# A two-layer decoder step on one core: the indexer's key tile first, unscaled values, and a head's key products in three PSUM banks

## Chip, cores and metric

One core of a Trainium2 chip runs the whole step in one launch. The metric is device time in microseconds (us), the median of several executions.

## What is computed

Two layers work on 512 prompt tokens and 8 samples of 4 new tokens (544 columns in all; 1024 channels, f32). Layer 0 mixes tokens by indexer-sparse attention, layer 1 by retention, and an MLP with squared relu follows each. Only layer 0's attention is touched by the change:

```python
z = h @ w_in                                   # 1024 -> 1024 q, 256 k, 256 v, 256 qi, 64 ki, 4 wi
q = rms_norm(q, q_gain); k = rms_norm(k, k_gain)
idx = jnp.einsum('thd,sd->ths', qi, ki)        # the indexer: 4 heads of 64
score = jnp.einsum('th,ths->ts', wi, relu(idx))
score = jnp.where(causal, score, -jnp.inf)
_, sel = lax.top_k(score, topk)                # topk = 128 keys of each query
logits = q . k[sel] * 128 ** -0.5 + bias       # 8 query heads on 2 key/value groups
y = (softmax(logits) @ v[sel]) @ w_out
```

`h` is the RMS-normed input, so each column (token) of the projection carries a factor r = rsqrt(mean square). The kernel multiplies by r after the projection, or leaves it out where a later norm removes it (queries and keys).

## The kernel before

**Dense tiles.** The projection gives transposed results: a tile holds 128 output channels (partitions) by 544 tokens, as two banks of 272 columns. f32 products are made from high and low parts (`wh`, `wl`, `xh`, `xl`; three products), so one tile is 8 steps of 6 matmuls, 48 in all (L506). The high part of a weight is made by ScalarE (L465), the low part by VectorE or, for keys, values and the first four query tiles, by GpSimd (L466). Tiles lie in the PSUM ring `mm`, which has two buffers of two banks. `ps_a` and `ps_b` have two buffers of one bank each.

**Order of the tiles.** The call at the end (`run(dense8(...) ...)`, L1174) lists them: two tiles of indexer queries (`ev_qi`), one narrow tile of 68 channels with the indexer's keys and head weights (`ev_kw`), two of keys (`ev_k`), two of values (`ev_v`), four of queries; after `settle()` a second `run(queries(1))` adds the other four queries. That makes 15 tiles, or 720 matmuls.

**What lies between them.** While `run` issues a tile it advances generators in a list `side`. `ev_kw` puts three of them there when the keys have been spread (L739) and transposed (L744): `ranks` (`scores`: the products L759 on TensorE, relu by ScalarE L762, weighted sum on VectorE L765 and L767), `deferred` (the samples' scores, L810 to L853) and `picks` (`select`: 16 rounds of MAX8 and MATCH_REPLACE on VectorE for each of three query blocks, L780 and L781). The samples' own selection, L865 to L871, has 16 rounds and a last one. All of it ends in the masks `nmask` and `nsel`.

**Values and keys.** `ev_v` multiplies the PSUM tile by r on VectorE (L914, `hs<-mm,RB`), TensorE transposes it (L897, L898) and ScalarE copies it to tokens (L899, L900). `ev_k` goes through `head_norm`, whose last VectorE product (L891) releases the transposes of the keys.

**Heads.** After the query tiles VectorE computes the query norms' reciprocal (L966), from which GpSimd and ScalarE make additive masks (L999, L1002), and `dq` (L969) for the samples' queries (L975, L977). `softmax` makes for each head four key products, one for each block of 128 queries, 512 to 128 keys wide (L1014); VectorE adds the mask and takes the row maximum out of PSUM (L1015), then L1017, the exponential on ScalarE (L1018), L1019 and L1020. `values` transposes the weights (L1030) and multiplies them with the values (L1041).

**Who sets the order.** The generators and the call's list only propose; a scheduler places every instruction when the program is built, from priorities and from buffers coming free. After that each engine runs its own fixed list. The chip sees nothing of the generators.

Of the kernel before, what the change touches and what calls it, by code (L numbers as in the profile page):

```python
# [26 lines left out]
FT = mybir.dt.float32  # L27
# [117 lines left out]
def decoder_step(ctx, tc, x_prompt, x_sample, cache_k, cache_v, cache_kidx, state_ret, page_table,  # L145
# [55 lines left out]
    def two(ap):  # L201
        return ap.rearrange("p (c n) -> p c n", c=2)
# [127 lines left out]

    def rsqrt_columns(x, n):
        return rsqrt(x, [tmp.tile([128, 20], FT, name=m)[:, :n] for m in ("rsy", "rsa")])

# [36 lines left out]
    def finish_norm(columns, then):  # L370
        if columns:
            ps = token_sums(acc)
            V.tensor_scalar(v1[:, :5], ps[:, :5], 1.0 / D, EPS, op0=OP.mult, op1=OP.add)
            r = rsqrt_columns(v1[:, :5], 5)
        else:
            r = row_rsqrt([acc] + late, D)
            late.clear()
        for _ in range(3):
            yield
        if columns:  # L380
            a, b = spread(r)
            A.activation(RB[:, :512], a, AF.Copy)
            V.tensor_copy(RB[:, 512:], b)
        else:
            spread_rows(r, RB)
        norm["pending"] = False
        if then:
            yield
            then()

    def start_norm(columns=False, then=None):
        norm["pending"] = True
        follow.append(finish_norm(columns, then))
# [103 lines left out]
    def tile_of(hl, xs, t, m, evac, i):  # L497
# [3 lines left out]
        for k in range(n):  # L501
# [8 lines left out]
            if k % 2:  # L510
                if k == n - 1:
                    if norm["pending"]:
                        z = PS["main"].tile([128, T], FT, name="early", tag=PS["early"][0], bufs=PS["early"][1])
                        A.activation(two(z), halves(ps), AF.Copy)
                        ps = z
# [152 lines left out]
    if True:  # L668
# [18 lines left out]
        SY.dma_start(ptab, page_table.rearrange("b n -> (b n)").rearrange("(o n) -> o n", o=1))  # L687
        start_norm(columns=True)

# [33 lines left out]
        def ev_qi(i, ps):  # L723
            V.tensor_tensor(two(qiT[i]), halves(ps), two(RB), op=OP.mult)
            yield
            for s in range(2):
                pq = ps_b()
# [6 lines left out]
        def ev_kw(i, ps):  # L734
# [13 lines left out]
            SY.dma_start(kidx_sample[0].rearrange("b t d -> (b t) d"), kitok[:NS, 4, :64])  # L748
            side.append([ranks, 2.0, 0.0])
            side.append([deferred, 0.7, 0.0])  # L750
            side.append([picks, 1.0, 0.0])

# [140 lines left out]

        def to_tokens(src, dst):
            pa, pb = ps_a(), ps_b()
            for b in range(4):
                PE.transpose(pa[:, 128 * b:128 * (b + 1)], src[:, 128 * b:128 * (b + 1)], ident)  # L897
            PE.transpose(pb[:NS, :128], src[:, SP:], ident)  # L898
            A.activation(dst[:, :4, :], pa.rearrange("p (b d) -> p b d", b=4), AF.Copy)  # L899
            A.activation(dst[:NS, 4, :], pb[:NS, :128], AF.Copy)  # L900

# [10 lines left out]
        def ev_v(g, ps):  # L912
            z = hs_tile(FT)
            V.tensor_tensor(two(z), halves(ps), two(RB), op=OP.mult)  # L914
            yield
            to_tokens(z, vtok[:, :, 128 * g:128 * (g + 1)])
            if g:
# [66 lines left out]
        def prompt_heads(hs):  # L984
# [19 lines left out]
            def softmax(h):  # L1004
                s = H[h]
                mx = tmp.tile([128, 4], FT, name="mx")
                sm = tmp.tile([128, 4], FT, name="sm")
                r = QR[h // 4][0][:, h % 4, :]
                for blk in (3, 2, 1, 0):
                    W = 128 * (blk + 1)  # L1010
                    c = slice(blk, blk + 1)
                    P = s["P"][blk]
                    ps = ps_a()
                    PE.matmul(ps[:, :W], qT[h][:, 128 * blk:128 * (blk + 1)], kT[h // 4][:, :W], start=True, stop=True)  # L1014
# [152 lines left out]
        def queries(g):  # L1167
# [5 lines left out]
        side.append([early, 0.7, 0.0])  # L1173
        run(dense8(w_in, 1536, 256, ev_qi) + dense8(w_in, 1792, 68, ev_kw, m=68) + dense8(w_in, 1024, 256, ev_k, eng=G)  # L1174
            + dense8(w_in, 1280, 256, ev_v, eng=G) + queries(0))
# [428 lines left out]
```

## Time and profile before

| | |
|---|---|
| median of 3 runs | 1584.08 us (1580.71 to 1584.30) |
| profiled execution, its own time | 1581.1 us |
| its span | 1579.2 us, mean granted clock 0.992 |
| PE (TensorE) busy | 1527.9 us, 97% |
| DVE (VectorE) busy | 1059.9 us, 67% |
| ACT (ScalarE) busy | 611.9 us, 39% |
| POOL (GpSimd) busy | 190.5 us, 12% |

Line numbers (L...) are those of this kernel. In rows that group instructions a following xN is their number; a product of plain f32 operands counts as two, a transpose or a split product as one. A bracket at a row's end gives the engine's idle time before it and what ended that. Time runs from the start of the span; the attention of layer 0 lies in the first 245 us.

### The profile page before, as it was taken

The page shows a single profiled execution, that of the slowest core. Times are in us where ns is not written, and L with a number is a line of the kernel's source. Part 1 is how long each engine was busy: PE and PEld are TensorE (multiplying, and loading weights), DVE is VectorE, ACT ScalarE, POOL GpSimd, SP SyncE. Part 2 cuts the span into 40 slices and gives each one's busy share as a digit, 9 for nine tenths or more (in the row PEclk, how much of TensorE's full clock was granted, in tenths as well). Part 3 has the DMA queues.
Part 4 walks back from the last instruction along what each step waited for, and adds up shares of the span by engine and source line. Part 5 has one row for each costly group of instructions (what it writes and reads, how often), then busy time and mean ns, then how long its engine had stood idle before and what let it go on. Part 6 is the DMA issues. An engine that isn't in the chain of part 4 may idle for free.

```text
span 1579.2 us, 28176 instructions
## 1 busy us (share of the span) xinstructions
PE 1527.9 (97%) x11670; PEld 1440.2 (91%) x11670; DVE 1059.9 (67%) x1950; ACT 611.9 (39%) x1036; POOL 190.5 (12%) x172
## 2 busy tenths in 40 slices
PE   7989899999999999999999999999998999999998
PEld 6689559899999999999899999999988999999998
DVE  6599774778677676556566465565568687677653
ACT  4423663545444444423232232223236454444432
POOL 3220320100000000212221122121210000000000
PEclk9999999999999999999999999999999999999999
DMA  6533252222332233223724622722812322332211
GB/s 177 156 98 94 71 185 81 81 81 81 107 107 86 82 101 107 79 79 109 246 67 163 197 84 91 260 71 73 274 60 64 105 83 82 107 107 82 83 51 57
DMA packets 135774, 172.53 MB, mean 109 GB/s; under 512 B 11660, under 2 KB 92630, under 8 KB 135646
## 3 DMA queue, kind: packets, MB, share of 16 engines
q1 hardware_dynamic: 135578, 170.72, 33.3%
q8 instruction: 91, 1.49, 0.4%
q14 instruction: 37, 0.30, 0.1%
q10 hardware_dynamic: 68, 0.02, 0.0%
HBM read 148.34 MB, written 25.01 MB: 110 GB/s over the span
## 4 chain that ended last, share of the span: by engine, by line
PE 87%; DVE 8%; DMA 2%; ACT 2%; issue 1%; SPq 0%; DVEq 0%; ACTq 0%
PE mm L506 56%; PE mm L570 16%; PE pa L570 2%; PE pb L1487 2%; PE pb L1513 1%; PE pa L1431 1%; DMA raw<-in_mlp_w_in_dram 1%; PE pa L1457 1%; DVE wl L466 1%; PE pb L1468 1%; PE pa L1041 1%; DVE sc L781 1%; PE pa L1014 1%; DVE m L780 1%; PE pb L1100 1%
## 5 line engine op out<-in xcount | busy, mean ns | idle before, releaser
L506 PE MATMUL mm<-xs,wh 128*128 128x272 f32 (+1 forms) x2784 | 501.4, 295 | 13.5 <-ACT r L1209 5.9
L506 PEld LDWEIGHTS mm<-xs,wh 128*128 128x128 f32 (+1 forms) x2784 | 410.0, 190 | 27.5 <-issue 8.9
L506 PE MATMUL mm<-hs,wh 128*128 128x272 f32 x2304 | 393.4, 289 | 3.2 <-DVE x L656 2.0
L506 PEld LDWEIGHTS mm<-hs,wh 128*128 128x128 f32 x2304 | 329.6, 189 | 5.5 <-DVE x L656 2.6
L465 ACT ACTIVATE wh<-raw 128x1024 fp32r<-128x1024 f32 x159 | 167.9, 1057 | 382.0 <-PE mm L506 356.9
L506 PE MATMUL mm<-xs,wl 128*128 128x272 f32 (+1 forms) x1392 | 297.5, 292 | 0.0
L570 PE MATMUL mm<-xs,sh 128*128 128x272 f32 x1344 | 259.1, 289 | 3.1 <-ACT r L583 1.8
L506 PE MATMUL mm<-hs,wl 128*128 128x272 f32 x1152 | 241.1, 288 | 0.0
L656 DVE TENSOR_TENSOR x<-mm,x 128x544 f32<-128x544 f32 x176 | 127.0, 723 | 163.4 <-PE mm L506 162.1
L506 PEld LDWEIGHTS mm<-xs,wl 128*128 128x128 f32 (+1 forms) x1392 | 222.7, 190 | 3.0 <-issue 1.1
L570 PEld LDWEIGHTS mm<-xs,sh 128*128 128x128 f32 x1344 | 210.3, 188 | 5.8 <-ACT r L586 3.5
L466 DVE TENSOR_TENSOR wl<-raw,wh 128x1024 fp32r<-128x1024 f32 x151 | 188.7, 1250 | 16.9 <-ACT wh L465 9.3
L570 PE MATMUL mm<-xs,sl 128*128 128x272 f32 x672 | 192.8, 287 | 0.0
L506 PEld LDWEIGHTS mm<-hs,wl 128*128 128x128 f32 x1152 | 182.1, 188 | 0.2
L570 PEld LDWEIGHTS mm<-xs,sl 128*128 128x128 f32 x672 | 126.3, 188 | 0.0
L662 ACT ACTIVATE sh<-ss 128x512 fp32r<-128x512 f32 x112 | 70.6, 630 | 123.8 <-PE mm L570 118.7
L663 DVE TENSOR_TENSOR sl<-ss,sh 128x512 fp32r<-128x512 f32 x112 | 76.7, 686 | 16.2 <-PE mm L570 16.2
L662 ACT ACTIVATE sh<-raw 128x512 fp32r<-128x512 f32 x84 | 53.1, 632 | 88.2 <-PE mm L570 70.8
L663 DVE TENSOR_TENSOR sl<-raw,sh 128x512 fp32r<-128x512 f32 x84 | 58.6, 698 | 9.3 <-PE mm L570 9.3
L1470 DVE SCALAR_TENSOR_TENSOR raw<-raw,pb 128x512 f32<-128x512 f32 x64 | 43.3, 684 | 24.9 <-PE pb L1468 15.8
L663 DVE TENSOR_TENSOR hs<-r,hs 128x544 fp32r<-128x544 f32 x64 | 46.1, 720 | 16.0 <-ACT hs L662 15.8
L412 POOL COPY acc<-sq 128x544 f32<-128x544 f32 x4 | 3.1, 780 | 444.8 <-ACT sq L408 444.8
(345 smaller groups left out, 1814.6 us busy)
## 6 DMA issues: line engine op xcount, KB each, us to landing
raw<-in_mlp_w_in_dram SPq DMA_DIRECT2D x32, 1024.0 KB
raw<-in_mlp_w_out_dram SPq DMA_DIRECT2D x32, 1024.0 KB
raw<-in_ret_w_in_dram SPq DMA_DIRECT2D x24, 1024.0 KB
raw<-in_state_ret_dram SPq DMA_DIRECT2D x32, 512.0 KB
out_dram<-raw SPq DMA_DIRECT2D x32, 512.0 KB
raw<-in_ret_w_out_dram SPq DMA_DIRECT2D x8, 1024.0 KB
raw<-in_att_w_in_dram SPq DMA_DIRECT2D x7, 1024.0 KB
raw<-in_cache_k_dram SPq DMA_DIRECT2D x32, 128.0 KB
```

The source lines that it names most:

```text
L465: A.activation(h, view, AF.Copy)
L466: eng.tensor_tensor(l, view, h.bitcast(FT), op=OP.subtract)
L506: PE.matmul(ps[:m, c, :HALF], w[:, k, m * t:m * (t + 1)], x[c] if isinstance(x, tuple) else x[:, HALF * c:HALF * (c + 1)], start=(k == 0 a ...
L570: PE.matmul(ps, a[:, i, :], b, start=(first and i == 0 and j == 0), stop=(i == 3 and j == 2), skip_group_check=True)
L656: V.tensor_tensor(two(xT[m]), halves(ps), two(xT[m]), op=OP.add)
L662: A.activation(dst_h, src, AF.Copy)
L663: V.tensor_tensor(dst_l, src, dst_h.bitcast(FT), op=OP.subtract)
L780: V.max(out=m8, in_=sc)
L781: V.match_replace(out=sc, in_to_replace=m8, in_values=sc, imm_value=TAKEN)
L1014: PE.matmul(ps[:, :W], qT[h][:, 128 * blk:128 * (blk + 1)], kT[h // 4][:, :W], start=True, stop=True)
L1470: V.scalar_tensor_tensor(sl, sl, gam4[h], pu, op0=OP.mult, op1=OP.add)
L1487: PE.matmul(ps[:, SP - WJ[j]:], v[:, j, 128 * e:128 * (e + 1)], a[:, AM[j]:AM[j] + WJ[j]], start=(j == 0 and v is vh and a is am[0]), stop ...
```

## The change

1. The token factor r of the first norm, as a column (`rsqrt_columns`), gets a tile of its own (`rcol`) that stays.
2. The narrow tile `ev_kw` is listed ahead of the two `ev_qi` tiles, and `ranks`, `deferred` and `picks` are put into `side` by the second of these.
3. `ev_v` copies the PSUM tile on ScalarE without the factor; after the transpose a token is a partition, so the factor is a scale of ScalarE's copy to tokens: five operations (four blocks and the samples) in place of two.
4. The four key products of a head lie in one `mm` buffer (blocks 3 and 2, a bank each) and one `ps_a` buffer (blocks 1 and 0 in one bank) instead of four `ps_a` buffers.

```diff
     def finish_norm(columns, then):
...
-            r = rsqrt_columns(v1[:, :5], 5)
+            r = rsqrt_columns(v1[:, :5], 5, columns)
...
-        start_norm(columns=True)
+        rcol = ap.tile([128, 5], FT, name="rcol")
+        start_norm(columns=rcol)
...
         def ev_qi(i, ps):
             V.tensor_tensor(two(qiT[i]), halves(ps), two(RB), op=OP.mult)
             yield
+            if i:
+                side.append([ranks, 2.0, 0.0])
+                side.append([deferred, 0.7, 0.0])
+                side.append([picks, 1.0, 0.0])
...
             SY.dma_start(kidx_sample[0].rearrange("b t d -> (b t) d"), kitok[:NS, 4, :64])
-            side.append([ranks, 2.0, 0.0])
-            side.append([deferred, 0.7, 0.0])
-            side.append([picks, 1.0, 0.0])
...
-        def to_tokens(src, dst):
+        def to_tokens(src, dst, scale=None):
...
-            A.activation(dst[:, :4, :], pa.rearrange("p (b d) -> p b d", b=4), AF.Copy)
-            A.activation(dst[:NS, 4, :], pb[:NS, :128], AF.Copy)
+            if scale is None:
+                A.activation(dst[:, :4, :], pa.rearrange("p (b d) -> p b d", b=4), AF.Copy)
+                A.activation(dst[:NS, 4, :], pb[:NS, :128], AF.Copy)
+                return
+            for b in range(4):
+                A.activation(dst[:, b, :], pa[:, 128 * b:128 * (b + 1)], AF.Identity, scale=scale[:, b:b + 1])
+            A.activation(dst[:NS, 4, :], pb[:NS, :128], AF.Identity, scale=scale[:NS, 4:5])
...
         def ev_v(g, ps):
             z = hs_tile(FT)
-            V.tensor_tensor(two(z), halves(ps), two(RB), op=OP.mult)
+            A.activation(two(z), halves(ps), AF.Copy)
             yield
-            to_tokens(z, vtok[:, :, 128 * g:128 * (g + 1)])
+            to_tokens(z, vtok[:, :, 128 * g:128 * (g + 1)], rcol)
...
+                pm, pq = ps_mm(), ps_a()
+                banks = {3: pm[:, 0, :512], 2: pm[:, 1, :384], 1: pq[:, :256], 0: pq[:, 256:384]}
                 for blk in (3, 2, 1, 0):
...
-                    ps = ps_a()
+                    ps = banks[blk]
...
-        run(dense8(w_in, 1536, 256, ev_qi) + dense8(w_in, 1792, 68, ev_kw, m=68) + dense8(w_in, 1024, 256, ev_k, eng=G)
+        run(dense8(w_in, 1792, 68, ev_kw, m=68) + dense8(w_in, 1536, 256, ev_qi) + dense8(w_in, 1024, 256, ev_k, eng=G)
```

The lists of instructions as placed, in three places. A name such as `mm_735` is one buffer of the ring `mm`; "waits" names the engine whose semaphore an instruction waits for. Lines of the changed kernel are a little higher: L507 is L506 before, L735 is L729, L762 is L759, L868 to L874 are L865 to L871, L974 and L977 are L966 and L969, L983 is L975, L985 is L977, L1024 and L1025 are L1014 and L1015, L1040 is L1030.

TensorE, the first scores. Before (the tile `mm_735` is the first of the keys, and the scores follow its end):

```order
L506 MATMUL mm_735<-xs_229,wh_481 128x272 x2
L506 MATMUL mm_735<-xs_230,wh_481 128x272 x2
L506 MATMUL mm_735<-xs_229,wl_482 128x272 x2
L506 MATMUL mm_735<-xs_244,wh_481 128x272 x2
L506 MATMUL mm_735<-xs_245,wh_481 128x272 x2
L506 MATMUL mm_735<-xs_244,wl_482 128x272 x2
L759 MATMUL pa_719<-hs_259,hs_256 128x512
L759 MATMUL pa_724<-hs_259,hs_256 128x512
```

Now (`mm_598` is the second tile of indexer queries):

```order
L507 MATMUL mm_598<-xs_244,wh_342 128x272 x2
L507 MATMUL mm_598<-xs_245,wh_342 128x272 x2
L507 MATMUL mm_598<-xs_244,wl_343 128x272 x2
L735 MATMUL pb_572<-hs_257,ca_126 128x32
L762 MATMUL pa_719<-hs_260,hs_257 128x512
L762 MATMUL pa_724<-hs_260,hs_257 128x512
L507 MATMUL mm_735<-xs_139,wh_491 128x272
```

The scores stand ahead of the first key tile instead of behind it: 144 dense matmuls come before the first score where 192 did.

VectorE, the end of the selection. Before:

```order
L865 MAX s_268<-ss 32x8
L966 RECIPROCAL qi_1688<-qr_1676 128x20
L969 TENSOR_TENSOR dq<-ident,qr_1676 32x128
L866 MATCH_REPLACE ss<-s_268,ss 32x544
L868 MAX s_268<-ss 32x8
L869 MEMSET s_268 32x7
L870 MATCH_REPLACE ss<-s_268,ss 32x552
L871 TENSOR_SCALAR nsel<-ss 32x544
L977 TENSOR_TENSOR Qs_275<-hs,pb 128x8x4 x4
L1015 ISA P,mx<-pa,P 128x512
```

Now:

```order
L872 MEMSET s_269 32x7
L327 SCALAR_TENSOR_TENSOR qw<-qw,qv 128x20
L873 MATCH_REPLACE ss<-s_269,ss 32x552
L328 SCALAR_TENSOR_TENSOR qr_1682<-qw,qr_1682 128x20
L874 TENSOR_SCALAR nsel<-ss 32x544
L974 RECIPROCAL qi_1694<-qr_1682 128x20
L977 TENSOR_TENSOR dq<-ident,qr_1682 32x128
L985 TENSOR_TENSOR Qs_276<-hs,pb 128x8x4 x4
L1025 ISA P,mx<-pa,P 128x256
```

The reciprocal, on which GpSimd's masks wait, stood before the samples' last selection operations and now stands behind them. Ahead of the first key tile's norm product (L891, now L894) there were 33 MAX8 in VectorE's list, and now there are 40.

TensorE, the boundary before the last two query tiles. Before, the last two tiles' matmuls follow one another, with two key products of head 0 some way ahead (`mm_1852` is the 13th tile, `mm_1973` the 14th):

```order
L506 MATMUL mm_1852<-xs_229,wl_1764 128x272 x2
L506 MATMUL mm_1852<-xs_244,wh_1763 128x272 x2
L506 MATMUL mm_1852<-xs_245,wh_1763 128x272 x2
L506 MATMUL mm_1852<-xs_244,wl_1764 128x272 x2
L506 MATMUL mm_1973<-xs_139,wh_1830 128x272 [waits PE_49,Activation_49]
L506 MATMUL mm_1973<-xs_139,wh_1830 128x272
```

Now (`mm_1875` and `mm_1941` hold key products of heads 0 and 1; `mm_1858` is the 13th tile, `mm_1977` the 14th):

```order
L507 MATMUL mm_1858<-xs_244,wl_1770 128x272 x2
L1024 MATMUL pa_1942<-kT0_270,hs_1503 128x256 [waits DVE_49]
L1024 MATMUL mm_1941<-kT0_270,hs_1503 128x512 [waits PE_49,Activation_49]
L983 MATMUL pb_1698<-dq_1696,ones_108 128x128 [waits DVE_49]
L1024 MATMUL pa_1876<-kT0_270,hs_1415 128x128 [waits DVE_49]
L1024 MATMUL mm_1875<-kT0_270,hs_1415 128x384 [waits DVE_49]
L1024 MATMUL pa_1942<-kT0_270,hs_1503 128x128 [waits DVE_49]
L507 MATMUL mm_1977<-xs_139,wh_1836 128x272 [waits DVE_49]
L507 MATMUL mm_1977<-xs_139,wh_1836 128x272
```

Two dense tiles (96 matmuls) moved behind `dq`, the products of heads 0 and 1 and VectorE's reading of them; both `mm` buffers are the heads' there.

## Rows read from the trace of the kernel before

**Rows 1.** The page of the profiled execution: its span, the busy time of the engines with their share of the span, and the shares by engine of the chain that ended last.

```profile
span 1579.2 us, 28176 instructions
...
PE 1527.9 (97%) x11670; PEld 1440.2 (91%) x11670; DVE 1059.9 (67%) x1950; ACT 611.9 (39%) x1036; POOL 190.5 (12%) x172
...
PE 87%; DVE 8%; DMA 2%; ACT 2%; issue 1%; SPq 0%; DVEq 0%; ACTq 0%
```

**Rows 2.** Busy time in four stretches (start and end in us, length; then busy us and instructions of PE, of its weight loads, of DVE, ACT and POOL; the granted TensorE clock as a share of full speed; DMA share; GB/s). 162.35 us is where DVE has read head 0's last key product; from 243.30 us on TensorE has only dense matmuls.

```profile
80.00:160.00 80.00, 73.68 (x556) 69.44 (x554) 79.75 (x225) 23.43 (x37) 15.01 (x13) 0.98 0.32 96
...
162.35:175.00 12.65, 10.41 (x43) 5.86 (x42) 11.15 (x41) 8.75 (x24) 6.36 (x9) 0.93 0.14 42
175.00:243.30 68.30, 62.62 (x430) 40.86 (x430) 47.38 (x190) 40.94 (x101) 14.21 (x20) 0.98 0.46 147
162.35:243.30 80.95, 73.02 (x472) 46.72 (x471) 58.53 (x230) 49.69 (x124) 20.56 (x29) 0.97 0.41 131
```

**Rows 3.** What PE waited for from 0 to 480 us, one line of the list: the instruction that waited and what released it, us in total, times, longest wait.

```profile
PE pa L1014 <- DVE mx L1015: 4.8, 5, 1.5
```

**Rows 4.** PE in order of time (start us, us from the first start to the last end, operation, count, idle before and its releaser): dense matmuls, the first value tile's transposes (96.06), dense matmuls behind them, and the first key tile's transposes (113.47).

```profile
90.86 0.66 PE L506 MATMUL mm<-xs,wh 128*128 128x272 f32 x4
91.36 0.41 PE L506 MATMUL mm<-xs,wl 128*128 128x272 f32 x2
91.61 0.29 PE L506 MATMUL mm<-xs,wh 128*128 128x272 f32 x1
96.06 1.11 PE L897 MATMUL pa<-ident,hs 128*128 128x128 f32 x4 [4.16 <-DVE hs L914]
...
97.04 1.03 PE L506 MATMUL mm<-xs,wh 128*128 128x272 f32 x3
...
113.47 0.63 PE L897 MATMUL pa<-ident,kT 128*128 128x128 f32 x4 [1.63 <-DVE kT L891]
```

**Rows 5.** PE, the same columns: the first two score products.

```profile
52.45 1.13 PE L759 MATMUL pa<-hs 64*128 64x512 f32 x4
```

**Rows 6.** DVE in order of time at the start of the indexer: the first score, two of its additions, the first score of the next block, the first MAX8.

```profile
54.24 1.87 DVE L765 TENSOR_SCALAR sc<-rl,kitok 128x512 f32<-128x512 f32 x1 [8.68 <-ACT rl L762]
...
56.52 1.61 DVE L767 SCALAR_TENSOR_TENSOR sc<-rl,kitok,sc 128x512 f32<-128x512 f32 x2
...
59.64 0.41 DVE L765 TENSOR_SCALAR sc<-rl,kitok 128x384 f32<-128x384 f32 x1
59.97 0.69 DVE L780 MAX8 m<-sc 128x8 f32<-128x512 f32 x1
```

**Rows 7.** DVE by form from 0 to 245 us: instructions, then busy us in total and mean ns of one, then idle time before them.

```profile
L1015 DVE CUSTOM_DVE_ANT_0 P<-pa,P 128x256 f32<-128x256 f32 x8 | 3.3, 414 | 0.4 <-PE pa L1014 0.3
L914 DVE TENSOR_TENSOR hs<-mm,RB 128x544 f32<-128x544 f32 x2 | 1.4, 694 | 0.0
```

**Rows 8.** DVE in order of time, end of the selection and the read of head 0's last key product.

```profile
154.21 0.25 DVE L966 RECIPROCAL qi<-qr 128x20 f32<-128x20 f32 x1
154.39 0.22 DVE L969 TENSOR_TENSOR dq<-ident,qr 32x128 f32<-32x128 f32 x1
...
157.02 1.23 DVE L871 TENSOR_SCALAR nsel<-ss 32x544 bf16<-32x544 f32 x1
...
162.14 0.29 DVE L1015 CUSTOM_DVE_ANT_0 P<-pa,P 128x128 f32<-128x128 f32 x1 [0.22 <-PE pa L1014]
```

**Rows 9.** POOL in order of time: the split of a weight operand while DVE selects, and the start of the mask work.

```profile
72.08 2.35 POOL L466 TENSOR_TENSOR wl<-raw,wh 128x1024 fp32r<-128x1024 f32 x1 [16.25 <-ACT wh L465]
...
154.56 1.63 POOL L999 TENSOR_SCALAR P<-strip,qi 128x256 f32<-128x256 f32 x4 [35.84 <-DVE qi L966]
156.15 5.48 POOL L1002 TENSOR_TENSOR P<-P,nmask 128x256 f32<-128x256 f32 x6
```

**Rows 10.** DVE in order of time: two operations beside splits of POOL, an addition of the first one's shape without a split beside it, and the first key tile's normed keys.

```profile
72.31 2.41 DVE L767 SCALAR_TENSOR_TENSOR sc<-rl,kitok,sc 128x256 f32<-128x256 f32 x1 [0.39 <-ACT rl L762]
...
75.77 0.46 DVE L767 SCALAR_TENSOR_TENSOR sc<-rl,kitok,sc 128x256 f32<-128x256 f32 x1
...
87.57 2.25 DVE L853 TENSOR_TENSOR ss<-ss,ca 32x32 f32<-32x32 f32 x1
...
112.60 0.72 DVE L891 SCALAR_TENSOR_TENSOR kT<-hs,gains,pa 128x512 f32<-128x512 f32 x1
```

**Rows 11.** PE in order of time: key products of the heads, the wait of the second half's query norms, and the first row with dense matmuls alone.

```profile
159.48 0.70 PE L1014 MATMUL pa<-kT,hs 128*128 128x256 f32 x2 [0.53 <-DVE mx L1015]
161.31 3.40 PE L1014 MATMUL pa<-kT,hs 128*128 128x128 f32 x6 [1.13 <-DVE mx L1015]
166.17 0.70 PE L1014 MATMUL pa<-kT,hs 128*128 128x256 f32 x2 [1.47 <-DVE mx L1015]
...
167.65 0.39 PE L1014 MATMUL pa<-kT,hs 128*128 128x128 f32 x2
...
170.70 1.02 PE L1014 MATMUL pa<-kT,hs 128*128 128x512 f32 x2
...
188.04 0.73 PE L975 MATMUL pb<-dq,ones 32*128 32x128 f32 x2 [2.04 <-DVE sm L1019]
...
217.73 0.81 PE L1014 MATMUL pa<-kT,hs 128*128 128x384 f32 x2
...
243.30 0.58 PE L506 MATMUL mm<-hs,wh 128*128 128x272 f32 x1
```

More of the change, by code (lines that the diff above doesn't have):

```diff
@@ L329, in rsqrt, with rsqrt_columns @@
         return y
-    def rsqrt_columns(x, n):
-        return rsqrt(x, [tmp.tile([128, 20], FT, name=m)[:, :n] for m in ("rsy", "rsa")])
+    def rsqrt_columns(x, n, y=None):
+        w = [tmp.tile([128, 20], FT, name=m)[:, :n] for m in (("rsa",) if y is not None else ("rsy", "rsa"))]
+        return rsqrt(x, w if y is None else [y] + w)
     QT = T // 4
@@ L370, in finish_norm @@
     def finish_norm(columns, then):
-        if columns:
+        if columns is not None:
             ps = token_sums(acc)
             V.tensor_scalar(v1[:, :5], ps[:, :5], 1.0 / D, EPS, op0=OP.mult, op1=OP.add)
-            r = rsqrt_columns(v1[:, :5], 5)
+            r = rsqrt_columns(v1[:, :5], 5, columns)
         else:
@@ L379, in finish_norm @@
             yield
-        if columns:
+        if columns is not None:
             a, b = spread(r)
@@ L389, in finish_norm, with start_norm @@
             then()
-    def start_norm(columns=False, then=None):
+    def start_norm(columns=None, then=None):
         norm["pending"] = True
@@ L513, in tile_of @@
                         z = PS["main"].tile([128, T], FT, name="early", tag=PS["early"][0], bufs=PS["early"][1])
-                        A.activation(two(z), halves(ps), AF.Copy)
+                        A.activation(two(z[:m]), halves(ps, slice(0, m)), AF.Copy)
                         ps = z
```

## The prediction, made before the changed kernel had run

> **What bounds the kernel now.** I read the page first: TensorE is busy for 97% of the span, and the chain that ended last lies on it for 87% and on VectorE for 8% [rows 1]. So time is gained only where TensorE waits, and these edits touch only the attention, the first 245 us. From 80 to 160 us VectorE is busy for 79.75 of 80 us and TensorE for 73.68 [rows 2]: VectorE's selection sets when the heads can start, and TensorE has the query tiles to fill the time with. After that it turns: from 162.35 us, where head 0's last key product has been read, to 243.30, where the heads are over, TensorE has 73.02 us of work and 7.93 us of idle time [rows 2]. I call these 80.95 us the tail. So two quantities decide: the moment M when head 0 has been read, and how much TensorE work and lost time come after M. The list of waits and TensorE's own rows name the places that the change aims at: 4.8 us in five waits of key products behind L1015 [rows 3], and one wait of 4.16 us behind L914 at the values [rows 4].
>
> **The keys' tile first.** The scores wait for 144 dense matmuls instead of 192. Six of them take 0.75 us (from 90.86 to 91.61) [rows 4], so 48 take 6.0 us, and the first score product moves from 52.45 [rows 5] to about 46.4. In the trace VectorE's first score operation loses a further 1.5 us: 512 keys take 1.87 us there, 384 take 0.41 [rows 6]. It ends together with a GpSimd split; 6 us earlier no split is under way. Together 7.5 us: the first MAX8 goes from 59.97 [rows 6] to about 52.5.
>
> **From there to the reciprocal (L966).** In VectorE's new list the two L914 are gone, 1.4 us [rows 7]. The samples' small operations (from 56.11 to 56.52) and the next block's first score (from 59.64 to 59.97) [rows 6], which stood ahead of the first MAX8, now stand behind it: +0.8 us. The reciprocal started at 154.21, 94.2 us after the first MAX8, in front of the last rounds of the samples' selection, which ended at 158.25; it now stands behind them, and less its own and `dq`'s 0.3 us that is +3.7 us [rows 8]. So it starts at 52.5 + 94.2 - 1.4 + 0.8 + 3.7 = 149.8, which is 4.4 us earlier and not 7.5. What follows it up to M, 8.1 us, I leave as long as it is, because GpSimd's mask work behind it (1.63 and 5.48 us in a row) [rows 9] is the same. M moves from 162.35 to 158.0.
>
> **Values.** The 4.16 us wait goes, with the slow stretch behind it: three matmuls took 1.03 us where four took 0.66 [rows 4], so half a microsecond. But through this stretch VectorE is the later of the two. TensorE then comes to the first key tile's transposes near 107 instead of 111.84 (113.47 less 1.63) [rows 4]. VectorE's product that they wait for, at 112.60 before [rows 10], comes hardly earlier: seven more rounds of selection stand ahead of it in the new list and use up the head start. So a wait of about 5 us moves from values to keys, and I cost the edit at nothing beyond VectorE's 1.4 us. ScalarE's three extra operations for each value tile lie where it has little to do (23.43 of 80 us) [rows 2]; were that cover gone they would cost under a microsecond a tile.
>
> **The boundary.** In TensorE's new list the last two dense tiles stand behind `dq` and the key products of heads 0 and 1. They were its cover during VectorE's selection, and now come after M. TensorE came to the products that need the selection at 158.95 (159.48 less 0.53) [rows 11]; without two tiles of 48 x 0.125 = 6.0 us each it comes there near 147 and waits for VectorE, with little in between, for some 9 us. That wait costs nothing by itself, since VectorE sets M. What it costs is 12.0 us of work moved into the tail.
>
> **The tail.** Of its 73.02 us of TensorE work 1.2 us are slowness: the six products at 161.31 took 3.40 us where such pairs took 1.02, 0.81 and 0.39 later [rows 11], and the granted clock up to 175 us was 0.93 [rows 2]. That leaves 71.8 us of work and 9.1 us lost. After the change the work is 71.8 + 12.0 - 1.5 = 82.3 us (1.5 us for three products of head 1 that are now done before M: 1.02, and about half a microsecond for the smaller ones). Of the lost time 3.4 us fall before 175 us (12.65 - 10.41, and the 1.2) [rows 2], where the heads have no other work beside them; now the two tiles lie there, and I take these as filled. After 175 us 1.7 us of L1015 waits are left (4.8 less 0.53, 1.13 and 1.47) [rows 3, 11]; with three of a head's products no longer in the ring that the value products use I take them as gone. 4.0 us stay lost, the 2.04 us at the second half's norms [rows 11] among them. The end is 158.0 + 82.3 + 4.0 = 244.3 us where it was 243.3: **1 us later, which is no change**. With nothing lost it would be 240.3, with all 9.1 us lost 249.4.
>
> The third bank brings a wait of its own. A 128-wide product waited up to 1.13 us for a buffer that L1015 still read [rows 11]; in the new list block 0's product waits in each head for VectorE's reading of block 1, which took 0.414 us [rows 7], since the two share a bank. By the rows I take most of that as hidden: dense matmuls or other heads' products stand between them, and nothing is added to the sum. If none of it hid, eight heads would pay 8 x 0.4 = 3.3 us, and the end would be 247.6.
>
> The Trainium skill ("PSUM — Partial Sum Buffer", section "PSUM bank collisions raise a hardware error") asks for TensorE and VectorE to be kept apart by bank and not by address, which speaks against packing two blocks into one bank; by that rule alone the sum would be the 247.6. The trace of before, where each product has a bank of its own, does not show it.
>
> **The rest.** `rcol`, the shorter early copy and the output transfers of the indexer's keys, which are issued earlier, lie on none of the chains named here; after the heads the two lists are alike, so nothing is added there.
>
> **The rivals.**
>
> *A. The head start comes through (faster).* While a GpSimd split ran from 72.08 to 74.43 [rows 9], a score addition took 2.41 us, and 0.46 without one; a small addition at 87.57 took 2.25 [rows 10]. By five splits between 60 and 120 us, four of them like this, VectorE loses some 8 us (an estimate from these rows). MAX8 and MATCH_REPLACE are not held, so it matters what stands beside a split, and that has changed everywhere. If two or three fewer are met, 5 us, M is at 153, and with the two tiles as cover 3 us are lost: 153 + 82.3 + 3 = 238.3, or -5 us: 1579. Against it: there are as many such operations in the list as before.
>
> *B. The two tiles are paid in full (slower).* Dense tiles and heads now want the same two `mm` buffers: a dense tile waits for a head's last read, and a head's products wait for a dense tile. Then nothing in the tail is filled and all 9.1 us stay lost: the end is 249.4, +6.1 us, 1590. It decides as soon as more than about 8 us are lost after M. For it: in the new list the 14th tile waits for VectorE, and both buffers are the heads' there. Against: such waits in the tail were 2.04 us at most [rows 11].
>
> *C. GpSimd holds more (slower, or no change).* If every one of the five splits is met in full, 2.3 us each, that is 11.5 instead of 8 us; M is 3.5 us later and the end 247.8, +4.5 us: 1588.5.
>
> The Trainium skill ("SBUF — State Buffer", section "Who interferes with whom") says that a VectorE instruction with two SBUF inputs contends with a GpSimd instruction that reads SBUF. The trace agrees: the 2.41 us row ends at 74.72, just behind the split's 74.43.
>
> *D. The removed waits count at face value (faster).* The 4.16 us at the values and the 1.7 us at the later heads go, and the two tiles find free room: -5.8 us, 1578. Against: VectorE is full through the first of these, so TensorE only waits elsewhere.
>
> **How the numbers follow.** A measurement of this kernel can tell about 0.3%, 4.75 us, from no change. The profiled execution took 1581.1 us, 3 us less than the median shown, 1584.08; the sum is a difference of two ends, which I add to the median: 1584.1 + 1.0 = **1585 us**. Chances: the forecast 0.40, A 0.20, B 0.18, C 0.12, D 0.10. The forecast's own spread is 4 us to each side, from 240.3 to about 248. The range, 1576.5 to 1592, takes in A and D with 1.5 us to spare below and B with 2 us above. Same is 0.43: most of the forecast, a third of A and a third of C. Faster is 0.28: the rest of A, D, and a little of the forecast. Slower is 0.29: B, the rest of C, and the forecast's upper end.
>
> **What would show it.** The wait behind L914 is gone; the first score product is near 46.4 us and the first MAX8 near 52.5; the keys' transposes wait about 5 us, to near 112; TensorE is idle for some 9 us ahead of the 14th dense tile, between 147 and 158; the reciprocal stands near 150. From there the tail tells the cases apart: the heads end near 244, by A or D under 240, by B over 248 with waits of dense tiles for L1015 or of key products for dense tiles. I am wrong in the first half if the reciprocal comes before 147 or after 153, and in the second if the time lost after M is under 2 or over 7 us.

## The result and the profile after

The changed kernel is slower: 1592.04 us (median of 9 runs, 1588.84 to 1594.0) against 1582.73 us (9 runs), ratio 1.0052 (95% interval 1.0039 to 1.0065), that is 8.2 us (6.2 to 10.3). I had forecast 1 us, no change; the upper end of my range lay at 1592.0, a hair under the measured time. Its profiled execution took 1590.35 us with a span of 1588.4.

The page after, the lines that answer to [rows 1]:

```profile
span 1588.4 us, 28179 instructions
...
PE 1535.0 (97%) x11670; PEld 1443.7 (91%) x11670; DVE 1061.7 (67%) x1948; ACT 614.7 (39%) x1044; POOL 191.0 (12%) x172
...
PE 86%; DVE 10%; DMA 2%; ACT 1%; issue 1%; POOL 0%; SPq 0%; DVEq 0%; ACTq 0%
```

The same stretches as in [rows 2], at the places that correspond: head 0's last key product is read at 162.40 (it was 162.35), and dense matmuls are alone from 252.95 (it was 243.30). Columns as there; the number behind the five busy times is the granted clock.

```profile
80.00:160.00 80.00, 68.03 (x477) 59.98 (x475) 78.17 (x222) 27.26 (x51) 16.93 (x15) 0.93 0.32 96
162.40:175.00 12.60, 12.53 (x73) 11.53 (x74) 5.30 (x26) 5.98 (x14) 2.92 (x6) 0.81 0.01 5
175.00:252.95 77.95, 72.79 (x494) 48.63 (x493) 51.92 (x201) 43.92 (x106) 15.93 (x22) 0.98 0.41 132
162.40:252.95 90.55, 85.32 (x565) 60.16 (x565) 57.22 (x227) 49.90 (x120) 18.85 (x27) 0.95 0.36 115
```

The heads end 9.65 us later, and from there to the end nothing more is lost (the span grew by 9.2). The tail grew from 80.95 to 90.55 us, and M, which I had put 4.4 us earlier, stayed where it was. TensorE is busy in the tail's first part for 12.53 of 12.60 us, so the two tiles do fill it; but at a granted clock of 0.81.

TensorE around the boundary, in order of time (start, us, operation, count, idle before):

```profile
148.00 0.59 PE L1024 MATMUL pa<-kT,hs 128*128 128x256 f32 x2
150.18 1.13 PE L1024 MATMUL mm<-kT,hs 128*128 128x512 f32 x2 [1.58 <-ACT hs L949]
152.93 0.48 PE L983 MATMUL pb<-dq,ones 32*128 32x128 f32 x2 [1.62 <-DVE dq L977]
155.62 0.79 PE L1024 MATMUL pa<-kT,hs 128*128 128x128 f32 x2 [2.20 <-DVE mx L1025]
157.00 1.65 PE L1024 MATMUL mm<-kT,hs 128*128 128x384 f32 x2 [0.58 <-DVE mx L1025]
160.23 0.80 PE L1024 MATMUL pa<-kT,hs 128*128 128x128 f32 x2 [1.59 <-DVE mx L1025]
162.47 1.28 PE L507 MATMUL mm<-xs,wh 128*128 128x272 f32 x4 [1.44 <-DVE mx L1025]
...
163.99 1.11 PE L507 MATMUL mm<-xs,wh 128*128 128x272 f32 x4
...
170.59 0.67 PE L507 MATMUL mm<-xs,wh 128*128 128x272 f32 x4
```

From 148 to 162.5 us TensorE runs six short products, five of them after a wait, where it had dense matmuls before; the sixth wait is that of the 14th tile, and the brackets add up to 9.0 us. It then begins the 14th tile at half speed: four matmuls take 1.11 us at 163.99 and 0.67 at 170.59. The same in windows of 10 us, after and then before:

```profile
150.00:160.00 10.00, 4.05 (x8) 1.59 (x8) 8.17 (x27) 5.67 (x13) 7.17 (x11) 0.67 0.53 157
160.00:170.00 10.00, 8.33 (x43) 7.77 (x44) 6.97 (x30) 3.85 (x11) 3.34 (x5) 0.64 0.09 29
```

```profile
150.00:160.00 10.00, 9.47 (x70) 8.55 (x69) 9.75 (x33) 4.81 (x8) 5.44 (x9) 1.00 0.55 169
160.00:170.00 10.00, 6.63 (x23) 3.58 (x23) 9.64 (x39) 6.22 (x17) 5.23 (x7) 0.83 0.11 34
```

VectorE after, where [rows 6, 8 and 10] stand before: the first MAX8, two operations held by GpSimd's splits, the end of the selection, the reciprocal, and head 0's last read.

```profile
53.62 0.69 DVE L783 MAX8 m<-sc 128x8 f32<-128x512 f32 x1
...
60.01 2.35 DVE L770 SCALAR_TENSOR_TENSOR sc<-rl,kitok,sc 128x384 f32<-128x384 f32 x1 [0.92 <-ACT rl L765]
...
105.86 2.26 DVE L326 TENSOR_TENSOR rsa<-rsy 128x5 f32<-128x5 f32 x1
...
152.11 0.43 DVE L874 TENSOR_SCALAR nsel<-ss 32x544 bf16<-32x544 f32 x1
152.47 0.26 DVE L974 RECIPROCAL qi<-qr 128x20 f32<-128x20 f32 x1
...
161.86 0.54 DVE L1025 CUSTOM_DVE_ANT_0 P<-mm,P 128x384 f32<-128x384 f32 x1
```

### The profile page after: what moved, and what is told of

The parts are those of the page before. It is cut to its first block, busy times and chain, and to the rows that moved or that the text cites. A ratio compares the mean times of both kernels' runs of the same rounds, so it can differ in the third digit from the quotient of the medians.

```text
span 1588.4 us, 28179 instructions
## 1 busy us (share of the span) xinstructions
PE 1535.0 (97%) x11670; PEld 1443.7 (91%) x11670; DVE 1061.7 (67%) x1948; ACT 614.7 (39%) x1044; POOL 191.0 (12%) x172
## 4 chain that ended last, share of the span: by engine, by line
PE 86%; DVE 10%; DMA 2%; ACT 1%; issue 1%; POOL 0%; SPq 0%; DVEq 0%; ACTq 0%
PE mm L507 55%; PE mm L571 16%; PE pa L571 2%; PE pb L1497 2%; PE pb L1523 1%; DVE sc L784 1%; PE pa L1441 1%; DVE m L783 1%; DVE wl L467 1%; PE pa L1467 1%; PE pb L1478 1%; PE pa L1051 1%; DMA raw<-in_mlp_w_in_dram 1%; PE mm L1024 1%; PE pb L1040 0%
## 5 line engine op out<-in xcount | busy, mean ns | idle before, releaser
L507 PE MATMUL mm<-xs,wh 128*128 128x272 f32 (+1 forms) x2784 | 505.9, 296 | 14.4 <-ACT r L1219 6.2
L507 PEld LDWEIGHTS mm<-xs,wh 128*128 128x128 f32 (+1 forms) x2784 | 412.1, 191 | 31.8 <-issue 11.9
L507 PE MATMUL mm<-hs,wh 128*128 128x272 f32 x2304 | 393.6, 289 | 3.2 <-DVE x L657 2.0
L507 PEld LDWEIGHTS mm<-hs,wh 128*128 128x128 f32 x2304 | 329.4, 189 | 5.1 <-DVE x L657 2.6
L466 ACT ACTIVATE wh<-raw 128x1024 fp32r<-128x1024 f32 (+1 forms) x159 | 168.0, 1057 | 380.8 <-PE mm L507 355.1
L507 PE MATMUL mm<-xs,wl 128*128 128x272 f32 (+1 forms) x1392 | 298.9, 293 | 0.1
L507 PE MATMUL mm<-hs,wl 128*128 128x272 f32 x1152 | 241.1, 288 | 0.0
L507 PEld LDWEIGHTS mm<-xs,wl 128*128 128x128 f32 (+1 forms) x1392 | 223.3, 190 | 3.8 <-issue 1.7
L467 DVE TENSOR_TENSOR wl<-raw,wh 128x1024 fp32r<-128x1024 f32 (+1 forms) x151 | 188.4, 1248 | 16.1 <-ACT wh L466 8.4
L507 PEld LDWEIGHTS mm<-hs,wl 128*128 128x128 f32 x1152 | 182.3, 189 | 0.2
```

The lines of the kernel that those rows point to most:

```text
L466: A.activation(h, view, AF.Copy)
L467: eng.tensor_tensor(l, view, h.bitcast(FT), op=OP.subtract)
L507: PE.matmul(ps[:m, c, :HALF], w[:, k, m * t:m * (t + 1)], x[c] if isinstance(x, tuple) else x[:, HALF * c:HALF * (c + 1)], start=(k == 0 a ...
```

## The experiments

Theory 1: the key products' new place alone costs the time, because it moves two dense tiles behind head 0, and the other two parts are worth little. Theory 2: the loss comes from the keys' tile first, with the slow stretch that the trace after has at 75 to 85 us (granted clock 0.75 from 70 to 80) and the splits of GpSimd. All ratios are to the kernel before, run on the same chip.

### Each part alone

**Key products in three banks, nothing else.** Against the kernel before:

```diff
+                pm, pq = ps_mm(), ps_a()
+                banks = {3: pm[:, 0, :512], 2: pm[:, 1, :384], 1: pq[:, :256], 0: pq[:, 256:384]}
...
-                    ps = ps_a()
+                    ps = banks[blk]
```

> The kernel before, with only the key products of a head in one mm and one pa buffer; tiles in the old order, values scaled by VectorE. Theory 1 (the banks part alone moves the last two query tiles behind head 0's reading, and the tail pays for them): 6 to 10 us slower than before (ratio 1.004 to 1.006), TensorE idle for 6 us or more ahead of the 14th dense tile, granted clock under 0.8 in the 20 us around it, and the tail after head 0's last read over 88 us. Theory 2 (the loss comes from the keys' tile first, through the slow stretch near 75 to 85 us and more GpSimd splits beside two-input operations): within 2 us of before.

Measured: 1.0074 (1.0054 to 1.0094), 11.7 us slower. The list has the boundary of the changed kernel, and so has the trace:

```profile
150.02 1.13 PE L1023 MATMUL mm<-kT,hs 128*128 128x512 f32 x2 [1.58 <-ACT hs L948]
156.94 0.79 PE L982 MATMUL pb<-dq,ones 32*128 32x128 f32 x2 [5.79 <-DVE dq L976]
159.94 0.80 PE L1023 MATMUL pa<-kT,hs 128*128 128x128 f32 x2 [2.21 <-DVE mx L1024]
161.95 1.65 PE L1023 MATMUL mm<-kT,hs 128*128 128x384 f32 x2 [1.21 <-DVE mx L1024]
163.56 0.79 PE L1023 MATMUL pa<-kT,hs 128*128 128x128 f32 x2
164.69 1.28 PE L507 MATMUL mm<-xs,wh 128*128 128x272 f32 x4 [0.34 <-DVE mx L1024]
```

This part alone costs all of the loss and more.

**Keys' tile first, nothing else** (the order of the tiles and the three lines moved from `ev_kw` to `ev_qi`).

> The kernel before with only the keys' tile first (values scaled by VectorE, four pa buffers). Theory 1: between 2 us slower and 2 us faster than before; the first MAX8 near 53.6 us, but the reciprocal no more than 2 us earlier than 154.2, because GpSimd's splits hold operations of VectorE for 10 us or more where they held them for 8, and because it stands behind the samples' selection. Theory 2: 4 us or more slower, with the granted clock near 0.75 from 75 to 85 us.

Measured: 0.9971 (0.9961 to 0.9981), 4.6 us faster, more than theory 1 gave it; the reciprocal at 149.20, 5.0 us earlier, which also missed. The granted clock was low near 67 to 74 us here, and the kernel is faster all the same, so theory 2 is wrong. Run a second time:

> The kernel with only the keys' tile first once more, beside the others on one chip: ratio to before 0.996 to 0.998, within 1.5 us of the kernel with three banks and late heads.

Measured: 0.9973 (0.9961 to 0.9985). The half clock came at 75 to 85 us in this execution, and the gain was the same.

**Values copied by ScalarE, nothing else** (`ev_v`, `to_tokens` and `rcol`).

> The kernel before with only the values copied by ScalarE and scaled behind the transposes. Theory 1: no wait of the values' transposes, a longer wait of the first key tile's transposes instead (3 to 6 us where it was 1.6), the reciprocal 0 to 2 us earlier, and the time within 2 us of before. A rival (the wait that goes counts at face value): 3.5 us or more faster.

Measured: 1.0025 (1.0012 to 1.0038), 4.0 us slower, outside both expectations. TensorE and then VectorE in its trace:

```profile
113.65 1.09 PE L899 MATMUL pa<-ident,kT 128*128 128x128 f32 x4 [7.32 <-DVE kT L893]
114.53 0.42 PE L900 MATMUL pb<-ident,kT 128*32 128x128 f32 x1
114.60 0.57 PE L507 MATMUL mm<-xs,wl 128*128 128x272 f32 x1
114.98 1.11 PE L507 MATMUL mm<-xs,wh 128*128 128x272 f32 x4
```

```profile
156.21 0.65 DVE L873 TENSOR_SCALAR nsel<-ss 32x544 bf16<-32x544 f32 x1
159.73 0.48 DVE L984 TENSOR_TENSOR Qs<-hs,pb 128x32 f32<-128x32 f32 x4 [2.88 <-PE pb L982]
```

The values' wait of 4.16 us and the keys' of 1.63 [rows 4] have become one of 7.32 at the keys, and half clock follows it. TensorE is some 1.8 us later behind it; the samples' product L982 stands behind all 720 dense matmuls in its list, so VectorE, though through with the selection 1.4 us earlier, now waits 2.88 us for TensorE, with the heads' reading queued behind. But in this execution that is made up again, as the rows that answer to those at 170.70 and 243.30 [rows 11] show:

```profile
170.78 1.02 PE L1021 MATMUL pa<-kT,hs 128*128 128x512 f32 x2
...
243.63 0.58 PE L507 MATMUL mm<-hs,wh 128*128 128x272 f32 x1
```

The heads end 0.33 us later, not 4.0, and the execution took 1582.98 us. Three of the twelve executions took 1591.0 to 1591.4 us at a mean granted clock of 0.984 to 0.985, the other nine 1582.8 to 1586.5 us at 0.988 to 0.992. No trace shows one of the three, so that this part costs 4.0 us is measured, and why is not shown.

**Keys first and values, without the banks** (the changed kernel with four `ps_a` buffers).

> The changed kernel with four pa buffers for a head's key products again: keys' tile first and values scaled by ScalarE stay. Theory 1: no dense tile behind the heads' products (the list has all 720 dense matmuls ahead of all but two key products); 1 to 4 us faster than before (ratio 0.9975 to 0.9995), since the reciprocal comes some 2 us earlier, though TensorE still has dense work then. Theory 2: 5 us or more slower than before, as the changed kernel is.

Measured: 1.0000 (0.9989 to 1.0010): neither. The two parts' -4.6 and +4.0 us cancel (with the keys' tile first, too, the values cost 4.6 us: 1.0000 against 0.9971); the loss of the whole change is the third part's. That the other two are worth little, as theory 1 had it, is true of their sum and not of either.

### How the third part costs

**No tile behind the heads.** The changed kernel with one condition more:

```diff
-            if hs[0] == 0:
-                yield 3.6
+            while "tiles" not in ready:
+                yield 0.5
...
         run(queries(1))
+        ready.add("tiles")
```

> The changed kernel, but the heads' products are first issued when the last query tile has been (a wait for a mark in the generator in place of its fixed lead). The list has all 720 dense matmuls ahead of the first key product. Theory 1 (what costs is that two dense tiles were moved behind head 0's reading): back to within 3 us of before (ratio 0.999 to 1.002), no long wait in front of the 14th tile, granted clock 1.0 from 140 to 155 us. Rival (the layout itself costs: heads and dense tiles sharing the ring of two, two blocks in one bank): 6 us or more slower than before still.

Measured: 0.9983 (0.9971 to 0.9994), 2.7 us faster than before and some 11 us faster than the changed kernel. All three parts are in it; only the order at the boundary is another. So neither the shared ring nor the shared bank costs this loss by itself.

**One tile behind the heads** (the mark set when the 14th tile has been issued):

```diff
         def ev_q(h, ps):
+            if h == 6:
+                ready.add("tiles")
```

> The changed kernel with the heads' products allowed from the moment when the 14th dense tile has been issued: in TensorE's list the 14th tile now comes before the samples' query norms and the reading of head 0, and only the last one behind them. Theory 1 (price of the moved dense tiles): about half of the change's loss is left, 2 to 6 us slower than before (ratio 1.001 to 1.004). Rival (what costs is any wait of TensorE there, whatever its length, or the sharing of the ring): the whole loss, ratio 1.005 or more. If the tiles were free where they are moved to: as the kernel with none moved, 0.998.

Measured: 0.9979 (0.9966 to 0.9991). My theory in the form "a price for each moved tile" fails: one is free, two cost 10 us or more. Its trace shows why. First its windows around the boundary, then the changed kernel's and the one before, over 140 to 165 us:

```profile
140.00:165.00 25.00, 25.00 (x178) 21.10 (x177) 21.60 (x71) 13.67 (x28) 10.61 (x15) 1.00 0.41 118
```

```profile
140.00:165.00 25.00, 15.98 (x83) 12.29 (x82) 22.71 (x77) 12.12 (x25) 10.51 (x15) 0.77 0.40 119
```

```profile
140.00:165.00 25.00, 23.05 (x148) 19.44 (x146) 24.49 (x78) 9.99 (x19) 10.44 (x15) 0.93 0.38 113
```

With the 14th tile in front, TensorE is busy until the reciprocal comes (151.38) and never waits: 25.00 of 25 us at full clock. The last tile, from 153.63 to 160.7 us, lies beside VectorE's reading of head 0 and fills that wait. With both tiles moved it stands idle for 9.0 us, and runs at 0.77 besides. What is paid for is not the work that moves but TensorE's time without work in front of it, and the half clock that came with it; how much either costs without the other, no run separates.

The changed kernel a second time, beside these runs:

> The changed kernel once more on the same chip as the one with a single tile moved: ratio to before 1.004 to 1.0065; the reciprocal between 150 and 155 us, and a half clock of 10 us or more around the boundary.

Measured: 1.0044 (1.0028 to 1.0059); the reciprocal at 155.25 in a profile that had half clock twice before 90 us, a little over the bound, and half clock for 13.7 us from 156.

**The combinations.** Keys first, three banks, values as before, heads late; its control with four `ps_a` buffers; and blocks 1 and 0 in a bank each.

```diff
-                pm, pq = ps_mm(), ps_a()
-                banks = {3: pm[:, 0, :512], 2: pm[:, 1, :384], 1: pq[:, :256], 0: pq[:, 256:384]}
+                pm, pq, pr = ps_mm(), ps_a(), ps_a()
+                banks = {3: pm[:, 0, :512], 2: pm[:, 1, :384], 1: pq[:, :256], 0: pr[:, :128]}
```

> Keys' tile first, key products in three banks, values as before, and the heads' products behind the last query tile. Theory 1: 2 to 8 us faster than before (ratio 0.995 to 0.999), as fast as the kernel with the keys' tile first alone or a little faster, since the waits of key products for L1015's line (4.8 us before) go. Rival (the layout costs by itself): slower than the next one by 4 us or more.

> The control for the one before: keys' tile first, four pa buffers, values as before, and the heads' products behind the last query tile. Theory 1: within 3 us of the kernel with the keys' tile first alone (ratio to before 0.995 to 0.999), with waits of key products for VectorE's reading of 3 us or more in total.

> Keys' tile first, values as before, heads behind the last query tile, but blocks 1 and 0 of a head in a bank each (one mm and two pa buffers). If block 0's wait for VectorE's reading of block 1 in the same bank costs its up to 0.4 us a head, this is 2 to 3 us faster than with the shared bank (ratio to before 0.995 to 0.996); if it hides, as I put it, within 1.5 us of it (0.996 to 0.998), or slower, since two more buffers of the ring that the value products use are taken.

Measured: 0.9971 (0.9956 to 0.9987), 0.9989 (0.9978 to 1.0001) and 0.9963 (0.9951 to 0.9975). With late heads the three banks come out some 2 to 3 us ahead of the control, but the intervals overlap, so that is not shown. Blocks 1 and 0 in a bank each are not told apart from blocks that share one: in both kernels key products in `mm` waited for VectorE's reading 1.7 us in total, at the same two places, and those in `ps_a` 0.2 us. Blocks 3 and 2 lie in one `mm` buffer in both. The last of these kernels, 5.9 us faster than before, is the fastest that I ran, though the intervals of four others reach it; it beats both the kernel before and the changed one.

**GpSimd's splits** (the changed kernel with `eng=V` for all tiles).

> The changed kernel with all low parts of weights made by VectorE, none by GpSimd. Theory C (splits of GpSimd hold two-input operations of VectorE for some 11 us, six of them): no such operation over 1.4 us before the reciprocal, and the reciprocal 2 to 5 us earlier than 152.47, though VectorE has about six more splits of 1.2 us ahead of it. By theory 1 the time moves by less than that: 1 to 4 us faster than the changed kernel (ratio to before 1.002 to 1.005), since the two tiles still come behind head 0. If theory C is wrong, the reciprocal comes 5 us or more later.

Measured: 1.0055 (1.0043 to 1.0067), the reciprocal at 155.32, later instead of earlier: a miss, and outside both accounts. VectorE's rows say how. Between the first MAX8 and the reciprocal the operations that are neither selection nor splits took 27.0 us in the changed kernel (69 of them, durations added up) and 15.7 here (67): some 11 us of holding are gone, as theory C had it. But ten splits instead of four stand there, 12.2 instead of 4.8 us, and VectorE was idle for 10.5 us instead of 1.6, 4.3 us of it between 66 and 80 us, where it waited for scores and for weights:

```profile
66.55 0.48 DVE L770 SCALAR_TENSOR_TENSOR sc<-rl,kitok,sc 128x256 f32<-128x256 f32 x1 [1.59 <-ACT rl L765]
...
72.04 0.49 DVE L770 SCALAR_TENSOR_TENSOR sc<-rl,kitok,sc 128x256 f32<-128x256 f32 x1 [1.53 <-ACT rl L765]
...
78.12 1.23 DVE L467 TENSOR_TENSOR wl<-raw,wh 128x1024 fp32r<-128x1024 f32 x1 [2.21 <-ACT wh L466]
```

TensorE ran at half clock from 70 to 76 us in that execution; how much of this idle time is the clock's and how much the list's, no run here separates.

Idle time and clock of TensorE from 140 to 165 us set the four rows with both tiles behind head 0 apart from all others; among the others they do not give the order:

| kernel | TensorE idle, us | granted clock | ratio to before |
|---|---|---|---|
| banks alone | 11.2 | 0.77 | 1.0074 |
| changed, splits on VectorE | 12.8 | 0.72 | 1.0055 |
| changed | 9.0 | 0.77 | 1.0052 |
| changed, again | 8.6 | 0.82 | 1.0044 |
| values alone | 2.3 | 1.00 | 1.0025 |
| before | 2.0 | 0.93 | 1 |
| keys and values | 2.8 | 0.99 | 1.0000 |
| keys alone, twice | 2.1, 2.6 | 1.00, 0.93 | 0.9971, 0.9973 |
| keys, late heads | 0.8 | 1.00 | 0.9989 |
| changed, late heads | 0.0 | 1.00 | 0.9983 |
| changed, one tile | 0.0 | 1.00 | 0.9979 |
| keys, three banks, late heads | 0.3 | 1.00 | 0.9971 |
| the same, four places | 1.1 | 1.00 | 0.9963 |

## Why the prediction was wrong in its size

The moves were all there: the end of the heads was forecast at 244.3 and came at 252.95. Of the 8.7 us between, 4.4 lie in M, which did not move, and the rest in the tail, where the lost time was put at 4.0 us and was 9.3. That the measured time still lies at the edge of the range is luck: the range reached there for rival B, which gives the price to another cause.

**The boundary is the step that failed.** I wrote that TensorE would wait for some 9 us and that this "costs nothing by itself, since VectorE sets M". The wait came as forecast (9.0 us in the brackets), the price did not. Up to the end of the heads TensorE has the same work in both kernels, so that end moves by what TensorE loses. After, from 140 to 170 us and over the half clock in it, and then before:

```profile
140.00:170.00 30.00, 20.98 (x113) 17.02 (x112) 25.14 (x87) 13.74 (x29) 10.51 (x15) 0.77 0.34 100
153.50:167.20 13.70, 7.97 (x27) 6.24 (x28) 10.80 (x39) 7.58 (x19) 9.84 (x14) 0.50 0.33 97
```

```profile
140.00:170.00 30.00, 26.10 (x164) 21.42 (x163) 29.39 (x101) 13.59 (x29) 10.67 (x15) 0.94 0.32 94
160.80:164.20 3.40, 2.89 (x5) 1.60 (x6) 3.18 (x11) 2.28 (x6) 3.40 (x5) 0.50 0.20 55
```

TensorE lost 9.0 us idle and half of the 7.97 us that it was busy at half clock, 4.0 us; before, 3.9 and 1.4. That is 7.7 us more, of the 9.65 us at the end of the heads. Outside this stretch little changed on balance: up to 140 us it waited 2.1 us less and lost 3.1 us more to half clock, and from 170 us on it was idle for 0.5 us less. The remaining 1.5 us or so these rows do not account for.

**The lost time after M** is the term of the sum in which this shows: 5.23 us idle, 2.4 us for the half clock up to 167.2 and 1.7 for a later one (238.8 to 242.2), 9.3 in all, where I had 4.0. By the same count it was 10.5 before: my 9.1 left out the second half-clock stretch of that kernel (188.1 to 191.5). So 1.2 us were filled and not 5.1. By my own sign (over 7 us lost after M) the second half of the prediction is wrong.

**The tail's work** was right: 82.3 forecast, 90.55 less 9.3 = 81.2 measured. The holes that I took as filled were filled (0.07 us idle up to 175 us, where 2.24 were), but the half clock behind the boundary wait took their place. I had counted the clock's price for the wait that goes and not for the one that comes.

**M** stayed at 162.40 instead of 158.0. The first MAX8 came at 53.62 (forecast 52.5): the first score product came at 44.77, but the fourth, behind more dense matmuls, at 50.74; and the first score operation stood beside a split of GpSimd again (1.63 us at 46.77, the split from 45.75), where I had written that none would be under way. From there to the reciprocal the operations beside selection and splits took 27.0 us where they took 23.6 before, which is rival C: operations of 1.39 to 2.35 us stood beside all six splits (60.01, 73.12, 93.60, 99.27, 105.86, 117.66), five with two inputs and, at 93.60, one with a single input. So the reciprocal came at 152.47 and not at 149.8; with the keys' tile first alone, where four operations were held, these took 24.3 us and it came at 149.20. And from it to M it was 9.9 us instead of 8.1. Block 2 of head 0 is now the last one read, but not for want of its product, which was done at 158.65: VectorE waited 1.20 us for a mask of GpSimd (155.13) and from then on was busy, with softmax operations beside GpSimd's mask work taking 1.08 us (L1030, 256 wide, at 158.76) and 1.46 (512 wide, at 160.48), where 256 wide took 0.34 at 163.69 behind that work.

**Right:** the wait behind L914 went, and a wait of 3.1 us (5 forecast) and one of 1.5 at the next norm took its place at the keys; in the kernels with one tile behind the heads and with keys and values, which had no half clock between 50 and 90 us, the keys' wait was 5.42 us. The removed waits did not count at face value (rival D). Costing the value edit at 1.4 us of gain was wrong: alone it cost 4.0 us, for a reason that stays open. The keys' tile first is worth 4.6 us by itself, near the 4.4 us that I had for M; in its trace head 0 has been read at 158.6, 3.7 us earlier than before.

**The rivals.** The time is that of B, 1590 to 1592, and more than 8 us were lost after M, as B has it. Its waits came too, each once, at the boundary: head 1's first product waited 1.58 us (150.18) until ScalarE had copied the 13th tile out of its `mm` buffer, and the 14th tile waited 1.44 us for VectorE. But these are 3.0 of the 9.0 us, and with the same sharing of the ring and late heads nothing is lost, so the sharing is not the price. I did not list a rival in which the boundary wait itself has a price.

**Shared buffers.** I took the wait of block 0 for VectorE's reading of block 1 as hidden. At the boundary it was not: 2.20 us (155.62) and 1.59 (160.23), 3.8 of the 9.0 us. Block 2 waited as well, 0.58 us (157.00), for the reading of block 3, which lies in the same `mm` buffer but in another bank; in all eight heads of this trace block 2's product starts behind that reading. The rule of the Trainium skill ("PSUM — Partial Sum Buffer", section "PSUM bank collisions raise a hardware error"), to guard by bank and not by address, asks for the first kind of wait; the second kind, between two banks, it does not ask for, so in this kernel the waits go by buffer. With late heads, where other work lay between, blocks 1 and 0 in one bank or two made no difference in the time.

## What to carry to other kernels

When an engine is the bound overall, a wait of it is not free because another engine sets the next moment there: count its idle time before the moment against the holes that are left behind it, and add the clock that the wait itself may bring. When work is moved behind a dependency, move as much as the wait in front of it leaves over and no more; here one tile was free and the second cost over 10 us. A buffer ring that two kinds of work share decides their order when the list is made, so read the list at the ring's boundaries before costing the layout.

## What the runs showed of the hardware

The granted clock fell to half (1.2 instead of 2.4 GHz) in or behind waits of 4.16 us [rows 4] and 7.32 us (values alone), and in the chain of short waits at the boundary. It came back after 3.4 us behind the first and after 6.8 us with the second; at the boundary, with short products between the waits, it stayed low for 13.7 us. In the wait of 3.13 us at the keys of the changed kernel it did not fall.

Half clock also came early, between 57 and 88 us, at places that differ from one execution to the next of one and the same kernel (67 to 74 us in one execution with the keys alone and 75 to 85 in the other), in a stretch of many short products with hardly a wait. What it costs there is not shown: in the changed kernel TensorE lost 4.7 us of work by it, and its next wait, at the keys, was shorter by 2.3 us than in the kernels without it.

The time of an execution goes with its granted clock: of the 31 executions of the kernel before on one chip those at 0.993 took 1578.7 to 1579.7 us, those at 0.987 and 0.988 took 1585.1 to 1587.3. All nine of the changed kernel lie at 0.984 to 0.987.

GpSimd's splits of 2.4 us (128x1024) held operations of VectorE that ran beside them, down to one of 128x5 that took 2.26 us (105.86); MAX8 beside a split took as long as without one (0.41 us for 256 columns and 0.67 for 512 in the kernel before).
